# A hybrid decoder layer on one core: value projection 512 wide, a fifth weight buffer, the first y loaded earlier, and the last product in two banks

## The chip, the cores and the metric

The kernel runs on one core of a Trainium2 chip. The metric is the device time in microseconds (us) of one execution; runs are given by their median and their spread. The engines are TensorE (PE in the profile, with its weight loads as PEld), VectorE (DVE), ScalarE (ACT), GpSimd (POOL) and SyncE (SP), whose queue issues all DMAs of this kernel.

## The reference

One decoder layer over x of 2048 rows and 1024 channels, in float32. One projection of x by w_in (1024 x 3584) feeds three branches; their outputs y_A, y_B, y_C (256, 256 and 512 wide) are joined, multiplied by w_out (1024 x 1024), added to the scaled input and normalised:

```python
h = einsum('bsd,de->bse', x, w_in)
a_u, a_v, a_g, b_val, b_glu, b_g, c_q, c_f, c_i, c_g = split(h)
y_a = sgu(gelu(a_u), layernorm(gelu(a_v))) * silu(a_g)     # chunks of 128, masked 128x128 per head
y_b = silu(layernorm(conv31(b_val * sigmoid(b_glu)))) * silu(b_g)
y_c = hgrn2(c_q, c_f, c_i) * silu(c_g)                     # gated recurrence, chunks of 64, 4 heads
x = layernorm(ALPHA * x + concat(y_a, y_b, y_c) @ w_out) * g + b
```

## The kernel before, in words

**Split arithmetic.** Every large product is made of three matmuls: each operand is split into a high part (a cast on ACT, L145) and a low part (a subtraction on VectorE, L146), and `three` (L198 to L201) multiplies high by high, high by low and low by high into one PSUM bank. `load_split` loads a raw tile of 128x512 by DMA (L151) and splits it. Weights go to the rings `whi` and `wlo`, four tiles of 128x1024 each; x goes to `xhi` and `xlo`.

**Projections.** `proj_f` puts weights on the stationary side and 512 tokens on the moving side: 24 matmuls of 128x512 into one of three "mm" banks. `proj_t` puts 128 tokens on the stationary side and 256 weight columns on the moving side: 24 matmuls of 128x256. It serves `sgu_values` (a_v) and `values` (c_i). `values` (L341 to L347) goes over the 512 columns of c_i in two passes `vp` of 256, over the two groups of 512 tokens in a half, and over the four tiles of 128 tokens in a group; after each tile ACT copies the bank's 256 columns to `vh`.

**Stages.** The rows are taken in two halves of 1024 tokens. In the first: branch B (GLU, convolution of 31 taps on VectorE, L280 and L283), branch A (`sgu`), the values, branch C (`hgrn_unit`, four heads). In the second: branch B, the values, branch C, and branch A last. `sgu_setup` (first half) makes the masked weights and `abias` of branch A with some constants.

**The combinations of w_out.** During the first half `wo_steps` makes seven sums of blocks of w_out (four k tiles each, 28 blocks in all): it loads `wr` (L686), subtracts (L697), splits into `wsh` and `wsl` (two buffers each), and stores both to DRAM (L679). The last stage uses them as `wob`. A step is due every 2.5 units of a program clock, `later` and `tick`, which each group of three matmuls advances. The order on each engine is then set by the framework's scheduler, which works on the program order and the buffers.

**The last stage.** It goes over eight row pairs p, each of two tiles of 128 rows (`r1`, `r2` in `xr`). Seven products of 12 matmuls replace eight: a11, a12, a22 are quarters of y, and s1 to s4 are sums of quarters. `y_steps(p)` is a generator: it loads four quarters `ry` from DRAM (L821) into the ring of raw tiles, splits pair a (a11, a12), makes s1, s2, s3 (L845 to L847) and splits pair s (s2, s3), makes s4 (L850) and splits pair t (s1, s4), and splits b (a22). In row pair p the steps of p+1 (`ahead`) lie between the products. `plus` (L910) and `join` (L913) add products to the rows of x, `normed` takes mean and variance on ACT (L885 to L888) and `rstd_of` on POOL (L225, L226), and `store` (L876 to L880) normalises in two VectorE operations, subtract the mean times g (L877), then scale and add b (L879), and writes out. The last pair has its own order and takes its statistics on VectorE (`stats`, L891 to L903); its last product a22 is done in two halves of 256 columns into one bank `poe`. `free_c` is called in the last branch A after each unit: it loads `wob` into freed memory and takes the first two steps of y of pair 0.

Of the kernel before, what the change touches and what calls it, by code (L numbers as in the profile page):

```python
# [11 lines left out]
F32 = mybir.dt.float32  # L12
# [71 lines left out]
def _body(tc, nc, d, ctx):  # L84
# [19 lines left out]

    warm = cst.tile([P, G], BF16, name="warm")
    nc.vector.memset(warm, 0.0)
    wps = bank("sc", 2, "wps")
    for _ in range(NWARM):
        nc.tensor.matmul(wps, warm[:, :P], warm, start=True, stop=True)

# [53 lines left out]
    def load_small(nm, srcs):  # L164
        hi = wp.tile([P, 1024], F32R, tag="whi", bufs=4, name=f"wh_{nm}")
        lo = wp.tile([P, 1024], F32R, tag="wlo", bufs=4, name=f"wl_{nm}")
        load_split(f"w{nm}", hi, lo, srcs)
        return hi, lo
# [172 lines left out]
    def values(hf, xs, vh):  # L341
        for vp in range(2):
            ws = [load_w(d["wt"][1 + vp, j], f"ci{hf}_{vp}_{j}") for j in range(2)]
            for gi in range(GPH):
                for tt in range(4):
                    pt = proj_t(ws, xs[gi], tt, f"ci{hf}_{vp}_{gi}_{tt}")
                    nc.scalar.copy(vh[:, gi * 4 + tt, vp * 256 : (vp + 1) * 256], pt[:, :256])  # L347

# [231 lines left out]

    def sgu_setup():
# [3 lines left out]
        ones = cst.tile([P, 64], F32, name="ones")  # L585
        nc.gpsimd.memset(ones, 1.0)
        sb = cst.tile([P, 2, P], F32, name="sgub")
        nc.sync.dma_start(sb, d["sgub"])
        pr = bank("sc", 2, "rowsum").rearrange("p (a t) -> p a t", t=P)
        for hd in range(4):  # L590
            nc.tensor.matmul(pr[64 * (hd % 2) : 64 * (hd % 2) + 64, hd // 2, :], ones,
                             wm[:, hd, :], start=True, stop=True)
        for ft in range(2):
            nc.vector.scalar_tensor_tensor(abias[:, ft, :], pr[:, ft, :], vcol(V_SLB + ft),
                                           sb[:, ft, :], ALU.mult, ALU.add)
# [17 lines left out]
    def sgu_unit(g, gi, x, pl, vhat, w, after):  # L613
        if True:
            for ft in range(2):
                nm = f"{ft}_{g}"
                pu = proj_f(w[2 * ft], x, f"u{nm}")
                gu = pl.tile([P, G], F32, tag="gu", bufs=2, name=f"gu{nm}")
                nc.scalar.activation(gu, pu, AF.Gelu_apprx_tanh)
                pg = proj_f(w[2 * ft + 1], x, f"ag{nm}")  # L620
                sg = pl.tile([P, G], F32, tag="ag", bufs=2, name=f"agt{nm}")
                nc.scalar.activation(sg, pg, AF.Silu)
# [25 lines left out]
    def first_loads():  # L648
        wt = [[wp.tile([P, 1024], F32R, tag=t, bufs=4, name=f"{t}_first{k}")
               for t in ("whi", "wlo")] for k in range(2)]  # L650
# [80 lines left out]
    def sgu(hf, xs, pl, after):  # L731
        ws = [load_w(d["wt"][0, j], f"av{hf}_{j}") for j in range(2)]
        vhat = sgu_values(hf, xs, pl, ws)
        w = [load_wf(o, hf) for o in (A_U, A_G, A_U + 1, A_G + 1)]
        for gi in range(GPH):
            sgu_unit(hf * GPH + gi, gi, xs[gi], pl, vhat, w, after)

    for hf in range(NHALF):
# [8 lines left out]
        if hf == 0:  # L747
            lower_bounds()
            sgu_setup()
            with ExitStack() as esw:  # L750
                wo_start(pool("wos", stack=esw, reuse_waits="tile"))
                with ExitStack() as esa:
                    pl = pool(f"a{hf}", stack=esa, reuse_waits="tile")
                    sgu(hf, xs, pl, lambda gi, ft: None)
                values(hf, xs, vh)
                assert wo_done
        else:
            assert live[0] == 0
            esc.close()
            values(hf, xs, vh)  # L760
# [40 lines left out]
    n0, n1 = slice(0, 512), slice(512, 1024)  # L801
    ys, xr, first_y = {}, {}, []
    xrp = pool("xr", stack=es, side="right", reuse_waits="tile")

    def load_xr(p):
        xr[p] = []
        for k in range(2):
# [3 lines left out]
            xr[p].append(r)  # L811

    stiles = pool("stiles", stack=es, side="right")

    def y_steps(p):
        raw = []
        for k in range(2):
            for e in range(2):
# [56 lines left out]

    def store(t, r, rs, mv, parts):  # L876
        nc.vector.scalar_tensor_tensor(r, r, mv[:, 0:1], gb[:, 0, :], ALU.subtract, ALU.mult)  # L877
        for ns in parts:
            nc.vector.scalar_tensor_tensor(r[:, ns], r[:, ns], rs, gb[:, 1, ns], ALU.mult, ALU.add)  # L879
            nc.sync.dma_start(d["out"][t * P : (t + 1) * P, ns], r[:, ns])  # L880

    def normed(t, r):
# [29 lines left out]
    def join(r, ns, t):  # L912
        nc.vector.tensor_add(r[:, ns], r[:, ns], t)  # L913
# [113 lines left out]
```

## Time and profile before

| what | value |
|---|---|
| three runs | 937.88, 940.69, 938.23 us; median 938.23 |
| profiled execution | 939.29 us, span 937.6 us |
| granted TensorE clock | 0.996 |
| instructions | 15803 |
| HBM | 75.00 MB read, 31.46 MB written |
| first half, branches B and A | 0 to 147 us |
| values of the first half | 147 to 196.9 us, with the second pass from 172 |
| values of the second half | 455 to 501 us |
| output product | 767 to 930 us |

The profile is one execution. A line of it gives the engine, the line of the kernel, the operation, the tile written and the tiles read. Groups give the number of instructions, busy time and the mean ns of one; in the timeline a row begins with the start and the duration, and ends with the idle time before it and what ended it. Matmuls overlap, so that their spacing, start to start, and not their printed duration, is what they cost. "PE a <- DVE b" in the list of waits means that TensorE, about to write a, stood until VectorE had written b.

### The profile page before, as it was taken

What the parts mean: (1) busy time and instruction counts of PE and PEld (TensorE: products, weight loads), DVE (VectorE), ACT (ScalarE), POOL (GpSimd) and SP (SyncE); (2) the same over time, 40 slices, a digit from 0 to 9 for tenths busy, and PEclk for the clock granted to TensorE, in tenths of its full rate; (3) what the DMA queues carried; (4) which work ended last, traced back from release to release, by engine and by line L of the source; (5) the groups of instructions that cost most, each with busy time, mean ns of one, the idle gap of its engine ahead of it and who ended that gap; (6) DMA issues with size and microseconds to landing.
All of it is one profiled execution on the core that took longest, in us unless ns stands there. A gap on an engine that the chain in (4) does not pass through costs nothing. (4 is left out here: it accounts for less than half of the span.)

```text
span 937.6 us, 15803 instructions
## 1 busy us (share of the span) xinstructions
PE 911.4 (97%) x6057; PEld 752.4 (80%) x6057; DVE 712.9 (76%) x1614; ACT 393.7 (42%) x790; POOL 76.6 (8%) x127
## 2 busy tenths in 40 slices
PE   8999999999999999999999999999999999999995
PEld 5789888987777777788998777777788887777884
DVE  6998899826787669897998767778765235888787
ACT  6644353234354446543323445344443343334450
POOL 0001101000010000010000000001012001121112
PEclk9999999999999999999999999999999999999998
DMA  8756464111112104411211111111322687455422
GB/s 269 264 180 239 157 235 141 68 46 35 35 46 68 46 23 158 135 57 35 68 46 46 45 46 46 46 45 46 121 83 68 229 322 260 131 182 179 155 91 90
DMA packets 60812, 107.48 MB, mean 115 GB/s; under 512 B 5312, under 2 KB 21952, under 8 KB 60608
## 3 DMA queue, kind: packets, MB, share of 16 engines
q1 hardware_dynamic: 60736, 106.48, 33.5%
q8 instruction: 47, 0.77, 0.4%
q14 instruction: 29, 0.24, 0.1%
HBM read 75.00 MB, written 31.46 MB: 114 GB/s over the span
## 5 line engine op out<-in xcount | busy, mean ns | idle before, releaser
L283 DVE SCALAR_TENSOR_TENSOR acc<-bh,vec,acc 128x512 f32<-128x512 f32 x240 | 172.2, 743 | 2.2
L146 DVE TENSOR_TENSOR wl<-rw,wh 128x512 fp32r<-128x512 f32 x84 | 56.6, 684 | 29.4 <-ACT wh L145 29.4
L145 ACT CAST wh<-rw 128x512 fp32r<-128x512 f32 x84 | 50.1, 620 | 31.2 <-PE pm_f L200 11.1
L199 PE MATMUL pm_ci<-wh_ci,xhix 128*128 128x256 f32 x192 | 54.5, 284 | 0.0
L200 PE MATMUL pm_ci<-wl_ci,xhix 128*128 128x256 f32 x192 | 54.3, 283 | 0.0
L201 PE MATMUL pm_ci<-wh_ci,xlox 128*128 128x256 f32 x192 | 54.3, 283 | 0.0
L550 ACT ACTIVATE jk<-po 128x128 f32<-128x128 f32 x64 | 17.8, 278 | 60.7 <-PE po L545 59.8
L199 PE MATMUL pm_f<-xhix,wh 128*128 128x512 f32 x96 | 41.2, 429 | 0.0
L199 PE MATMUL pm_q<-xhix,wh 128*128 128x512 f32 x96 | 41.0, 427 | 0.0
L347 ACT COPY vh<-pm_ci 128x256 f32<-128x256 f32 x32 | 11.9, 373 | 65.6 <-PE pm_ci L201 65.6
L199 PE MATMUL pm_cg<-xhix,wh 128*128 128x512 f32 x96 | 39.0, 407 | 0.0
L200 PE MATMUL pm_q<-xlox,wh 128*128 128x512 f32 x96 | 39.0, 406 | 0.0
L201 PE MATMUL pm_q<-xhix,wl 128*128 128x512 f32 x96 | 37.9, 394 | 0.0
L201 PE MATMUL pm_f<-xhix,wl 128*128 128x512 f32 x96 | 37.8, 393 | 0.0
L200 PE MATMUL pm_f<-xlox,wh 128*128 128x512 f32 x96 | 37.6, 392 | 0.0
L201 PE MATMUL pm_cg<-xhix,wl 128*128 128x512 f32 x96 | 37.6, 392 | 0.0
L200 PE MATMUL pm_cg<-xlox,wh 128*128 128x512 f32 x96 | 37.5, 390 | 0.0
L199 PEld LDWEIGHTS pm_ci<-wh_ci,xhix 128*128 128x128 f32 x192 | 36.9, 192 | 0.0
L200 PEld LDWEIGHTS pm_ci<-wl_ci,xhix 128*128 128x128 f32 x192 | 36.9, 192 | 0.0
L201 PEld LDWEIGHTS pm_ci<-wh_ci,xlox 128*128 128x128 f32 x192 | 36.9, 192 | 0.0
L225 POOL TENSOR_SCALAR crs<-ss 128x4 f32<-128x4 f32 x16 | 3.6, 226 | 373.8 <-ACT jk L550 373.8
L438 DVE COPY_PREDICATED ST<-msk,sc 64x192 f32<-64x192 int32 (+2 forms) x96 | 28.8, 300 | 5.5 <-PE sc L432 3.2
(348 smaller groups left out, 2789.1 us busy)
## 6 DMA issues: line engine op xcount, KB each, us to landing
rw<-wf SPq DMA_DIRECT2D x84, 256.0 KB, 3.0
wob<-wo_dr SPq DMA_DIRECT2D x14, 1024.0 KB, 11.6
xr<-x SPq DMA_DIRECT2D x16, 512.0 KB, 4.5
ry<-y_dr SPq DMA_DIRECT2D x32, 256.0 KB, 3.9
out<-xr SPq DMA_DIRECT2D x15, 512.0 KB, 2.6
wo_dr<-wsh SPq DMA_DIRECT2D x28, 256.0 KB, 3.5
wo_dr<-wsl SPq DMA_DIRECT2D x28, 256.0 KB, 2.5
rx<-xT SPq DMA_DIRECT2D x24, 256.0 KB, 3.3
```

The lines of the kernel that those rows point to most:

```text
L145: nc.scalar.copy(hi, src)
L146: nc.vector.tensor_sub(lo, src, hi.bitcast(F32))
L199: nc.tensor.matmul(out, wh, xh, start=first, stop=False, **kw)
L200: nc.tensor.matmul(out, wh, xl, start=False, stop=False, **kw)
L201: nc.tensor.matmul(out, wl, xh, start=False, stop=last, **kw)
L225: nc.gpsimd.tensor_scalar(r, mv_var, scale, EPS, ALU.mult, ALU.add)
L283: nc.vector.scalar_tensor_tensor(a, h[:, k : k + G], vcol(cw + k), a, ALU.mult, ALU.add)
L347: nc.scalar.copy(vh[:, gi * 4 + tt, vp * 256 : (vp + 1) * 256], pt[:, :256])
L438: nc.vector.copy_predicated(ST[rr, :, 64 * m + j0 * b : 64 * m + (j0 + nj) * b], msk[rr, mo : mo + mw].unsqueeze(1).to_broadcast([64, 4, mw]),
L550: nc.scalar.activation(jk, po[:, c * P : (c + 1) * P], AF.Square, accum_out=ss[:, c : c + 1])
```

## The change

It has five parts.

1. `values` makes one pass of 512 columns with 128x512 matmuls. Its four weight tiles hold two k tiles of 512 columns each (`wi`, a new layout made on the host; `wt` keeps a_v).
2. The rings `whi` and `wlo` have five tiles (WB). The memory comes from the warm-up tile, `ones` and `sgub`, which go to pools of their own (`warm`, `sgs`) that are released; from `gu` and `ag`, which get one buffer; and from the DMA scratch, 1024 in place of 2048. The pool of the w_out combinations, opened next, takes over memory of `sgs`.
3. `y_steps` yields after its loads. Row pair 0 is loaded and its pair a split after the first unit of the last branch A, its pairs s and t follow after the third, where pair 1 is loaded too. In the loop the loads of p+2 are issued at the end of p.
4. The halves of the last a22 go to two banks, `poe` and `pof`.
5. `store` becomes `centre` and `finish`. In the last pair r1's `finish` stands behind the aggregate of r2 in the program.

```diff
+WB = 5
-        for vp in range(2):
-            ws = [load_w(d["wt"][1 + vp, j], f"ci{hf}_{vp}_{j}") for j in range(2)]
-            for gi in range(GPH):
-                for tt in range(4):
-                    pt = proj_t(ws, xs[gi], tt, f"ci{hf}_{vp}_{gi}_{tt}")
-                    nc.scalar.copy(vh[:, gi * 4 + tt, vp * 256 : (vp + 1) * 256], pt[:, :256])
+        ws = [load_w(d["wi"][j], f"ci{hf}_{j}") for j in range(4)]
+        for gi in range(GPH):
+            for tt in range(4):
+                pt = bank("mm", 3, f"pm_ci{hf}_{gi}_{tt}")
+                xs_ = slice(tt * P, (tt + 1) * P)
+                for kt in range(KT):
+                    wh, wl = [t.rearrange("p (k f) -> p k f", f=G)[:, kt % 2, :]
+                              for t in ws[kt // 2]]
+                    three(pt, xs[gi][0][:, kt, xs_], xs[gi][1][:, kt, xs_], wh, wl,
+                          kt == 0, kt == KT - 1)
+                    tick(0.64)
+                nc.scalar.copy(vh[:, gi * 4 + tt, :], pt)
...
-            sgu_setup()
+            with ExitStack() as est:
+                sgu_setup(pool("sgs", stack=est, reuse_waits="tile"))
...
-            if gi == 1:
-                first_y.append(y_steps(0))
-                for _ in range(2):
-                    next(first_y[0])
+            if gi == 0:
+                first_y.extend(y_steps(p) for p in range(2))
+                next(first_y[0])
+                next(first_y[0])
+            else:
+                next(first_y[0])
+                next(first_y[0])
+                next(first_y[1])
...
-        ahead = y_steps(p + 1)
+        ahead = first_y.pop(0) if first_y else None
...
             normed(2 * p, r1)
             if p + 2 < NP:
+                first_y.append(y_steps(p + 2))
+                next(first_y[0])
                 load_xr(p + 2)
...
-            d2 = bank("sc", 2, f"poe{p}")
+            d2 = bank("sc", 2, f"poe{p}"), bank("tr", 1, f"pof{p}")
...
-            store(2 * p, r1, rs1, mv1, [slice(0, DM)])
+            centre(r1, mv1)
             for k, ns in enumerate(halves):
-                product(d2, y["a22"], 6, True, ns)
-                join(r2, ns, d2[:, ns])
+                product(d2[k], y["a22"], 6, True, ns)
+                join(r2, ns, d2[k][:, ns])
                 take2(k + 1)
             rs2, mv2 = done2()
-            store(2 * p + 1, r2, rs2, mv2, (n0, n1))
+            finish(2 * p, r1, rs1, [slice(0, DM)])
+            centre(r2, mv2)
+            finish(2 * p + 1, r2, rs2, (n0, n1))
```

More of the change, by code (lines that the diff above doesn't have):

```diff
@@ L103, in bank @@
         return t
[L105 to L109, printed above, removed]
+    with ExitStack() as esw:
+        warm = pool("warm", stack=esw, side="right", reuse_waits="tile").tile([P, G], BF16, name="warm")
+        nc.vector.memset(warm, 0.0)
+        wps = bank("sc", 2, "wps")
+        for _ in range(NWARM):
+            nc.tensor.matmul(wps, warm[:, :P], warm, start=True, stop=True)
     ident = cst.tile([P, P], F32, name="ident")
@@ L164, in load_small @@
     def load_small(nm, srcs):
-        hi = wp.tile([P, 1024], F32R, tag="whi", bufs=4, name=f"wh_{nm}")
-        lo = wp.tile([P, 1024], F32R, tag="wlo", bufs=4, name=f"wl_{nm}")
+        hi = wp.tile([P, 1024], F32R, tag="whi", bufs=WB, name=f"wh_{nm}")
+        lo = wp.tile([P, 1024], F32R, tag="wlo", bufs=WB, name=f"wl_{nm}")
         load_split(f"w{nm}", hi, lo, srcs)
@@ L579, in _body, with sgu_setup @@
     abias = cst.tile([P, 2, P], F32, name="abias")
-    def sgu_setup():
+    def sgu_setup(tp):
         nc.sync.dma_start(wm, d["sguw"])
@@ L584, in sgu_setup @@
                                 fill=0.0, base=0, channel_multiplier=-1)
-        ones = cst.tile([P, 64], F32, name="ones")
+        ones = tp.tile([P, 64], F32, name="ones")
         nc.gpsimd.memset(ones, 1.0)
-        sb = cst.tile([P, 2, P], F32, name="sgub")
+        sb = tp.tile([P, 2, P], F32, name="sgub")
         nc.sync.dma_start(sb, d["sgub"])
@@ L617, in sgu_unit @@
                 pu = proj_f(w[2 * ft], x, f"u{nm}")
-                gu = pl.tile([P, G], F32, tag="gu", bufs=2, name=f"gu{nm}")
+                gu = pl.tile([P, G], F32, tag="gu", bufs=1, name=f"gu{nm}")
                 nc.scalar.activation(gu, pu, AF.Gelu_apprx_tanh)
                 pg = proj_f(w[2 * ft + 1], x, f"ag{nm}")
-                sg = pl.tile([P, G], F32, tag="ag", bufs=2, name=f"agt{nm}")
+                sg = pl.tile([P, G], F32, tag="ag", bufs=1, name=f"agt{nm}")
                 nc.scalar.activation(sg, pg, AF.Silu)
@@ L648, in first_loads @@
     def first_loads():
-        wt = [[wp.tile([P, 1024], F32R, tag=t, bufs=4, name=f"{t}_first{k}")
+        wt = [[wp.tile([P, 1024], F32R, tag=t, bufs=WB, name=f"{t}_first{k}")
                for t in ("whi", "wlo")] for k in range(2)]
@@ L731, in sgu @@
     def sgu(hf, xs, pl, after):
-        ws = [load_w(d["wt"][0, j], f"av{hf}_{j}") for j in range(2)]
+        ws = [load_w(d["wt"][j], f"av{hf}_{j}") for j in range(2)]
         vhat = sgu_values(hf, xs, pl, ws)
@@ L801, in _body @@
     n0, n1 = slice(0, 512), slice(512, 1024)
-    ys, xr, first_y = {}, {}, []
+    ys, xr, first_y, stiles = {}, {}, [], []
     xrp = pool("xr", stack=es, side="right", reuse_waits="tile")
@@ L811, in load_xr @@
             xr[p].append(r)
-    stiles = pool("stiles", stack=es, side="right")
     def y_steps(p):
@@ L824, in y_steps @@
                 raw.append(r)
+        yield
         a11, a12, a21, a22 = raw
@@ L828, in pair @@
         def pair(nm, srcs, names):
-            hi = wp.tile([P, 1024], F32R, tag="whi", bufs=4, name=f"wh_y{p}_{nm}")
-            lo = wp.tile([P, 1024], F32R, tag="wlo", bufs=4, name=f"wl_y{p}_{nm}")
+            hi = wp.tile([P, 1024], F32R, tag="whi", bufs=WB, name=f"wh_y{p}_{nm}")
+            lo = wp.tile([P, 1024], F32R, tag="wlo", bufs=WB, name=f"wl_y{p}_{nm}")
             n = srcs[0].shape[1]
@@ L837, in pair @@
                 out[name] = [t[:, sl].rearrange("p (k t) -> p k t", t=P) for t in (hi, lo)]
-        sa = stiles.tile([P, 1024], F32, tag="ysum", bufs=2, name=f"ysa{p}")
-        sb = stiles.tile([P, 1024], F32, tag="ysum", bufs=2, name=f"ysb{p}")
+        pair("a", (a11, a12), ("a11", "a12"))
+        yield
+        sa = stiles[0].tile([P, 1024], F32, tag="ysum", bufs=2, name=f"ysa{p}")
+        sb = stiles[0].tile([P, 1024], F32, tag="ysum", bufs=2, name=f"ysb{p}")
         s2, s3 = sa[:, :512], sa[:, 512:]
         s1, s4 = sb[:, :512], sb[:, 512:]
-        pair("a", (a11, a12), ("a11", "a12"))
-        yield
         nc.vector.tensor_add(s1, a21, a22)
@@ L853, in y_steps @@
         pair("b", (a22,), ("a22",))
+    stiles.append(pool("stiles", stack=es, side="right"))
     load_xr(0)
@@ L859, in _body @@
         sgu(NHALF - 1, xs, pl, free_c)
-    for _ in first_y[0]:
+    ot = pool("ot", stack=es, side="right", reuse_waits="tile")
+    for _ in first_y.pop(0):
         pass
-    ot = pool("ot", stack=es, side="right", reuse_waits="tile")
     gb = ot.tile([P, 2, DM], F32, name="gb")
@@ L874, in product, with centre, finish @@
             tick(0.64)
-    def store(t, r, rs, mv, parts):
+    def centre(r, mv):
         nc.vector.scalar_tensor_tensor(r, r, mv[:, 0:1], gb[:, 0, :], ALU.subtract, ALU.mult)
+    def finish(t, r, rs, parts):
         for ns in parts:
@@ L888, in normed @@
         nc.scalar.activation(jk, r, AF.Square, bias=nm, accum_out=mv[:, 1:2])
-        store(t, r, rstd_of(smp, mv[:, 1:2], 1, "ors", 1.0 / DM), mv, [slice(0, DM)])
+        rs = rstd_of(smp, mv[:, 1:2], 1, "ors", 1.0 / DM)
+        centre(r, mv)
+        finish(t, r, rs, [slice(0, DM)])
     def stats(t, r, parts):
@@ L982 @@
     "wf": ((NFT, P, KT * P), F32),
-    "wt": ((3, 2, P, 4 * 256), F32),
+    "wt": ((2, P, 4 * 256), F32),
+    "wi": ((4, P, 2 * 512), F32),
     "wout": ((P, KT, DM), F32),
@@ L1009 @@
         "wf": c(w.reshape(KT, P, NFT, P).transpose(2, 1, 0, 3).reshape(NFT, P, KT * P)),
-        "wt": c(tok.reshape(3, 2, 4, P, 256).transpose(0, 1, 3, 2, 4).reshape(3, 2, P, 1024)),
+        "wt": c(w[:, 256:512].reshape(2, 4, P, 256).transpose(0, 2, 1, 3).reshape(2, P, 1024)),
+        "wi": c(w[:, C_I * P : C_G * P].reshape(4, 2, P, 512).transpose(0, 2, 1, 3)
+                .reshape(4, P, 1024)),
         "wout": c(np.asarray(w_out)[0].reshape(KT, P, DM).transpose(1, 0, 2)),
@@ L1019 @@
     nc = _bacc.Bacc("TRN2", target_bir_lowering=False, num_devices=1,
-                    dynamic_dma_scratch_size=2048)
+                    dynamic_dma_scratch_size=1024)
     d = {n: nc.dram_tensor(n, s, t, kind="ExternalInput").ap() for n, (s, t) in _INS.items()}
```

1 line of the change is left out of this document (removed).

## The prediction

> **What bounds the kernel now.** I read the page first, then busy time by stage, then the waits of TensorE, then the timeline at the places that the change touches. The page's head and TensorE's row:
>
> ```profile
> span 937.6 us, 15803 instructions
> PE 911.4 (97%) x6057; PEld 752.4 (80%) x6057; DVE 712.9 (76%) x1614; ACT 393.7 (42%) x790; POOL 76.6 (8%) x127
> ```
>
> TensorE is busy 97% of the span, so time can come out in two ways only: fewer microseconds of matmul, or fewer of the 26 us in which it stands. Busy time by stage (columns: busy us and count on PE, PEld, DVE, ACT, POOL, then clock, DMA share, GB/s), for branch B's end with branch A and the weight combinations, for the eight row pairs of the output product, and for the end:
>
> ```profile
> 37.00:172.00 135.00, 133.51 (x817) 116.67 (x816) 127.08 (x225) 58.10 (x91) 12.41 (x23) 1.00 0.54 186
> ...
> 766.90:923.20 156.30, 153.42 (x665) 122.84 (x662) 119.50 (x153) 61.44 (x107) 23.41 (x28) 1.00 0.50 166
> 923.20:937.60 14.40, 3.53 (x25) 3.03 (x23) 8.96 (x16) 0.00 (x0) 3.04 (x2) 0.71 0.19 73
> ```
>
> The clock is 1.00 until the end, so nothing here hangs on it. TensorE's last 14.4 us hold 3.5 us of work: that stage is bound by the chain of the last row pair. In branch A, VectorE is nearly full too (127 of 135 us). The waits of TensorE that lie where the change works:
>
> ```profile
> PE poe L199 <- DVE xr L913: 3.2, 1, 3.2
> ...
> PE poz L199 <- DVE xr L910: 1.6, 2, 1.2
> ...
> PE pm_glu L200 <- DVE xlox L146: 1.0, 1, 1.0
> ...
> PE pod L201 <- DVE wl_y_s L146: 0.5, 1, 0.5
> ...
> PE pod L199 <- DMA wob<-wo_dr: 0.4, 1, 0.4
> ```
>
> **Values 512 wide.** 768 matmuls of 128x256 become 384 of 128x512 (the same columns in all), and 32 copies become 16. TensorE's timeline where the values end and the next projection begins, and in the output product, then the row of the copies:
>
> ```profile
> 194.76 0.28 PE L199 MATMUL pm_ci<-wh_ci,xhix 128*128 128x256 f32 x1
> ...
> 196.93 0.40 PE L199 MATMUL pm_f<-xhi_first,wh 128*128 128x512 f32 x1
> ...
> 197.62 0.40 PE L199 MATMUL pm_f<-xhi_first,wh 128*128 128x512 f32 x1
> 789.10 0.39 PE L199 MATMUL poz<-wob,wh_y_a 128*128 128x512 f32 x1
> ...
> 792.27 0.39 PE L201 MATMUL poa<-wob,wl_y_a 128*128 128x512 f32 x1
> L347 ACT COPY vh<-pm_ci 128x256 f32<-128x256 f32 x32 | 11.9, 373 | 65.6 <-PE pm_ci L201 65.6
> ```
>
> The length that a row prints (0.28, 0.40) overlaps the next matmul; what counts is start to start. From 194.76 to 196.93 are 18 matmuls: 2.17 / 18 = 0.1206 us each. 512 wide, from 196.93 to 197.62 are 3: 0.230; from 789.10 to 792.27 are 14: 0.2264. A 512-wide one thus costs about 12 ns less than two halves. Now 768 x 0.1206 = 92.6 us; then 384 x 0.230 = 88.3 or x 0.2264 = 86.9. The middle, 87.6, gives **-5.0** (bounds -4.3 and -5.7). All of it lies on the path, as TensorE does not wait in the values. The copies become about 0.6 us long (a 128x512 cast on ACT takes 0.62, row below), eight per half; three banks of 24 x 0.228 = 5.5 us hide them.
>
> [...]
>
> The four weights of the values now stay in use to the last tile, where two came free half way. The fifth buffer takes branch C's first weight ahead; the second is split after the values, two casts and two subtractions (0.62 and 0.68 each by the rows below, 2.6 us), behind the 5.5 us of the first projection. Zero; without that cover 2.6 us per half.
>
> **Start of branch B.** The `wos` pool takes over the memory of `sgs`, so the first load of w_out waits until `abias` is made. SyncE's order at the start, before:
>
> ```order
> L151 DMA rx_4_284<-xT 128x512
> L582 DMA wm<-sguw 128x512
> L588 DMA sgub<-sgub 128x256
> L151 DMA rx_5_284<-xT 128x512
> L686 DMA wr_0_658<-wout 128x1024
> L151 DMA rx_6_288<-xT 128x512
> L151 DMA rx_7_292<-xT 128x512
> ```
>
> and after:
>
> ```order
> L590 DMA wm<-sguw 128x512
> L596 DMA sgub<-sgub 128x256
> L153 DMA rx_5_288<-xT 128x512
> L153 DMA rx_6_292<-xT 128x512
> L153 DMA rx_7_296<-xT 128x512
> L153 DMA rw_0_0_397<-wf 128x512
> ```
>
> The last two x tiles no longer stand behind a 512 KB load. What that load does now, by the timelines of TensorE, SyncE, ACT and VectorE:
>
> ```profile
> 30.02 0.50 PE L200 MATMUL pm_glu<-xlox,whi_first 128*128 128x512 f32 x1 [0.98 <-DVE xlox L146]
> 19.33 0.43 SPq L686 DMA_DIRECT2D wr<-wout  x1
> 25.44 0.62 ACT L145 CAST wsh<-wr 128x512 fp32r<-128x512 f32 x1 [0.62 <-DMA wr<-wout]
> 26.75 0.68 DVE L146 TENSOR_TENSOR wsl<-wr,wsh 128x512 fp32r<-128x512 f32 x1
> ...
> 28.02 0.68 DVE L697 TENSOR_TENSOR wtb<-wr 128x512 f32<-128x512 f32 x1
> ...
> 29.28 1.28 DVE L146 TENSOR_TENSOR xlox<-rx,xhix 128x512 fp32r<-128x512 f32 x2
> ```
>
> xlox 6 and 7 come at 29.28 behind 1.4 us of w_out work and the wait for it, and TensorE stands 0.98 us before 30.02. Without w_out ahead they come over 1.2 us earlier: **-1.0** (bounds 0, if the x transfers are late by themselves, and -1.3, with a slower restart).
>
> In exchange all 28 blocks of w_out (cast, subtraction, two stores) fall between about 80 and 148 us, where 18 fall now. I price that at zero: TensorE waits for ACT's evictions there, which stand in the same queue as the casts, and three banks cover them. Its bound above is the slower rival.
>
> **y early, and the fifth buffer in the product.** The y of row pair 0 is loaded and split inside branch A, that of pair 1 is loaded there, and later ones a pair earlier. SyncE has a queue of these loads now, and TensorE two stalls at the first change of pair:
>
> ```profile
> 775.00 18.01 SPq L821 DMA_DIRECT2D ry<-y_dr  x6
> 794.10 0.50 PE L201 MATMUL pod<-wob,wl_y_s 128*128 128x512 f32 x1 [0.53 <-DVE wl_y_s L146]
> 798.83 0.50 PE L199 MATMUL poz<-wob,wh_y_s 128*128 128x512 f32 x1 [1.24 <-DVE xr L910]
> 796.90 1.28 DVE L877 SCALAR_TENSOR_TENSOR xr<-xr,omv,gb 128x1024 f32<-128x1024 f32 x1
> 798.10 0.68 DVE L910 SCALAR_TENSOR_TENSOR xr<-xr,poz 128x512 f32<-128x512 f32 x1
> ```
>
> VectorE's order in row pair 0 (xr_7232 and xr_7234 are its rows, xr_7236 the first row of pair 1), before:
>
> ```order
> L910 SCALAR_TENSOR_TENSOR xr_7234<-xr_7234,poz_8118 128x512 x2
> L913 TENSOR_TENSOR xr_7234<-xr_7234,pod_8120 128x512 x2
> L910 SCALAR_TENSOR_TENSOR xr_7232<-xr_7232,poz_8118 128x512
> L845 TENSOR_TENSOR ysb_8155<-ry_1_0_8150,ry_1_1_8152 128x512
> L847 TENSOR_TENSOR ysa_8154<-ry_0_0_8146,ry_1_0_8150 128x512
> L846 TENSOR_TENSOR ysa_8154<-ysb_8155,ry_0_0_8146 128x512
> L877 SCALAR_TENSOR_TENSOR xr_7234<-xr_7234,omv_8222,gb 128x1024
> L850 TENSOR_TENSOR ysb_8155<-ry_0_1_8148,ysa_8154 128x512
> L146 TENSOR_TENSOR wl_y_s<-ysa_8154,wh_y_s 128x1024
> ```
>
> and after (xr_6824 and xr_6826; pair 1's sums stand ahead of all this):
>
> ```order
> L926 SCALAR_TENSOR_TENSOR xr_6824<-xr_6824,poz_7718 128x512
> L929 TENSOR_TENSOR xr_6824<-xr_6824,poa_7719 128x512
> L148 TENSOR_TENSOR wl_y_s<-ysa_7778,wh_y_s 128x1024
> L926 SCALAR_TENSOR_TENSOR xr_6826<-xr_6826,poz_7718 128x512
> L148 TENSOR_TENSOR wl_y_t<-ysb_7779,wh_y_t 128x1024
> L926 SCALAR_TENSOR_TENSOR xr_6826<-xr_6826,poz_7718 128x512
> L929 TENSOR_TENSOR xr_6826<-xr_6826,pod_7720 128x512 x2
> ```
>
> wl_y_s of pair 1 is ready before pair 0's last products, and the four sums no longer lie between pair 0's joins and pair 1. That removes the waits at 794.10 and 798.83, 0.53 + 1.24 = 1.8 us. The stage has 156.3 us for some 660 matmuls of 0.228, which is 150.5: 5.8 us of stalls in all. The fifth buffer lets a pair's first split start without waiting for a buffer of the pair before. VectorE has 119.50 / 8 = 14.9 us of work per pair against TensorE's 84 x 0.228 = 19.15, so a pair can run almost without a stall where the order lets it. I take **-3.5**: the 1.8 and some two fifths of the other 4.0 (bounds -5.5, and +1 if the new order costs 0.15 a pair and gives nothing back). Pair 0's own splits move into branch A's second half: a few us of ACT and VectorE there, hidden as long as both have room, and at most the 1.8 back if they have none. The 0.4 for wob stays. `gu` and `agt` with one buffer each are rewritten a whole unit later, two projections of 5.5 us: zero.
>
> **The last product.** Timelines of VectorE, TensorE and POOL at the end:
>
> ```profile
> 926.33 1.27 DVE L879 SCALAR_TENSOR_TENSOR xr<-xr,orl,gb 128x1024 f32<-128x1024 f32 x1
> 927.51 0.41 DVE L913 TENSOR_TENSOR xr<-xr,poe 128x256 f32<-128x256 f32 x1
> 927.96 0.43 DVE L895 BATCH_NORM_STATS2 ost<-xr 128x6 f32<-128x256 f32 x1
> 927.98 0.39 PE L199 MATMUL poe<-wob,wh_y_b 128*128 128x256 f32 x1 [3.22 <-DVE xr L913]
> 930.00 0.42 DVE L913 TENSOR_TENSOR xr<-xr,poe 128x256 f32<-128x256 f32 x1 [1.61 <-PE poe L201]
> 930.91 0.24 DVE L899 BATCH_NORM_AGGREGATE omv<-ost 128x2 f32<-128x18 f32 x1
> 931.18 0.15 DVE L901 TENSOR_SCALAR orl<-omv 128x1 f32<-128x1 f32 x1
> 931.41 1.52 POOL L902 TENSOR_TENSOR orl<-orl,nhalf 128x1 f32<-128x1 f32 x1 [6.39 <-DVE orl L901]
> 932.97 1.41 DVE L879 SCALAR_TENSOR_TENSOR xr<-xr,orl,gb 128x512 f32<-128x512 f32 x2 [0.44 <-POOL orl L902]
> ```
>
> The second half waits for the join of the first, as both lie in one bank. VectorE's order there after the change:
>
> ```order
> L911 BN_STATS ost_8788<-xr_8640 128x6
> L929 TENSOR_TENSOR xr_8640<-xr_8640,poe_8790 128x256
> L929 TENSOR_TENSOR xr_8640<-xr_8640,pof_8791 128x256
> L911 BN_STATS ost_8788<-xr_8640 128x6 x2
> L893 SCALAR_TENSOR_TENSOR xr_8638<-xr_8638,orl_8861,gb 128x1024
> L915 BN_AGGR omv_8909<-ost_8788 128x2
> L917 TENSOR_SCALAR orl_8911<-omv_8909 128x1
> L889 SCALAR_TENSOR_TENSOR xr_8640<-xr_8640,omv_8909,gb 128x1024
> L893 SCALAR_TENSOR_TENSOR xr_8640<-xr_8640,orl_8911,gb 128x512 x2
> ```
>
> With two banks TensorE goes on at once, 3.2 us earlier at about 924.8, and is done at about 926.7; but row 1's L893 (1.2 us) now stands ahead of the aggregate. From 926.33: two joins at 0.45 (927.23), two stats at 0.46 (928.15), L893 (929.35), aggregate and epsilon 0.5 (929.85), POOL 1.52 and the hand-over (931.44), where 932.97 stands now: **-1.5** (bounds -0.8 if joins wait for TensorE, -2.2). Of the 3.2 us, about half is kept by VectorE's queue.
>
> **Sum.** -5.0 - 1.0 - 3.5 - 1.5 = -11.0. The profiled execution took 939.29 (span 937.6 and 1.7 around it), so 928.3; it stands 1.06 over the median of 938.23, so about **927.2** for the median.
>
> **Rivals.**
> 1. *The w_out blocks hold up branch A* (slower). From the trace's groups of wsh and its stores, of abias, and ACT's last gate:
>
> ```profile
> L679 SPq DMA_DIRECT2D wo_dr<-wsh x28: 319/353/1368, 32.2 to 140.3; - x28
> DMA to landing us min/median/max: 2.0/3.5/5.2
> 76.15 0.60 DVE L594 SCALAR_TENSOR_TENSOR abias<-rowsum,vec,sgub 128x128 f32<-128x128 f32 x2
> 148.31 0.60 ACT L622 ACTIVATE agt<-pm_ag 128x512 f32<-128x512 f32 x1
> ```
>
>    The first load goes out at 77 and lands about 82 (an estimate, with the longest landing). A block waits for the store of the block two before: 0.62 + 0.35 + 3.5 = 4.5 us for two, and 28 take 63 us, to 145: in time for the last agt (148.31), which stands behind the last block in ACT's order. At the longest landing it is 6.2 for two, to 168. Two banks of cover are 11 us, so it decides from (148 + 11 - 82) / 28 = 2.75 us per block. At 3.3 per block (174) TensorE would stand 15 us: **942**. For it: VectorE's full stage and the heavier DMA traffic. Against: the median landing. Chance 0.09.
> 2. *The product's pace is VectorE's.* If in each pair one 1.28 us operation falls ahead of the plus that frees poz, as at 796.90 now, TensorE loses 1.3 in seven pairs, +9 in place of -3.5: **939.5**. For it: VectorE's operations come in long pieces, and its order is fixed. Against: the four us of room per pair. Chance 0.07.
> 3. *The early y is hidden anyway*: the stalls move to another wait, the product gains 0 to 1 us. **930**. Chance 0.18.
> 4. *The 12 ns are not a matmul's own*: they come from something that both widths share per column, and one of 512 costs what two of 256 do. The values save nothing, **932**. The rows at two places contradict it; chance 0.04. [...]
>
> My forecast has 0.60, and 0.02 is left for gains elsewhere. About 0.3%, 2.8 us, is what a measurement here can tell from no change. Faster by more: 0.60 + 0.18 + 0.04 + 0.02 = 0.84; same (rival 2): 0.07; slower (rival 1): 0.09. The terms' lower ends add to -14.7, their upper ends to -4.1; with 1 us on each side for small stalls elsewhere that is 922.5 to 935, with rivals 3 and 4 inside and the first two outside (0.16).
>
> **What would show it.** Right: pm_ci 128x512 some 0.228 apart, 384 of them; no wait of 1 us for xlox near 30; poe's wait on L913 gone and the last L893 some 1.5 us nearer to the start of the last product; the product stage near 152.8 us. Wrong: TensorE waiting for ACT's gu or agt between 100 and 160 us (rival 1), for xr at every change of pair (rival 2), or the value stage not shorter by over 4 us (rival 4).

## The result, and the profile after

Over six runs each, the kernel before takes 939.13 us (937.55 to 940.69) and the changed one 934.38 us (933.51 to 935.1): a ratio of 0.9949, with a 95% interval of 0.9934 to 0.9964. That is 4.75 us faster, where 11.0 was forecast. The profiled execution takes 934.35 us with a span of 932.6, so 5.0 us of span against before.

Where they come from is seen by cutting both spans at the first matmul of each stage on TensorE (`pm_ci`, the first `pm_f` behind it, `poz`, `poe`):

| stage, us | before | after | difference | forecast |
|---|---|---|---|---|
| start to the first values | 147.53 | 146.62 | -0.9 | -1.0 |
| values, first half | 49.40 | 53.78 | **+4.4** | -2.5 |
| branch C, then branch B of the second half | 258.23 | 258.25 | 0 | 0 |
| values, second half | 46.07 | 43.52 | -2.5 | -2.5 |
| branches C and A, second half | 265.72 | 266.54 | +0.8 | 0 |
| output product, to `poe` | 156.22 | 151.64 | -4.6 | -3.5 |
| `poe` to the end | 14.41 | 12.27 | -2.1 | -1.5 |
| span | 937.58 | 932.61 | -5.0 | -11.0 |

Two stages went against the forecast. Branches C and A of the second half lost 0.8 us. The first half's values should have become 2.5 us shorter and became 4.4 longer, 6.9 us off: more than the whole shortfall of 6.0. The 0.9 us of the start can't be put down to the change: in another profile of the changed kernel (e11 below) the start takes 147.9 us, and in e4, which starts like the kernel before, 146.7. The waits of TensorE in the changed kernel, and the one that the kernel before has in the values:

```profile
PE bb L330 <- DVE bhn L324: 3.5, 1, 3.5
PE pst L531 <- DVE s L537: 2.7, 5, 0.9
...
PE pm_ci L202 <- DVE wl_ci L148: 1.2, 2, 1.0
...
PE pm_ci L201 <- ACT wh_ci L147: 1.0, 1, 1.0
```

```profile
PE bb L328 <- DVE bhn L322: 1.4, 1, 1.4
```

poe, poz, pod on wl_y_s and pm_glu on xlox are gone, as forecast. New are two waits of the values for their own weights, wh_ci and wl_ci, and the wait for bhn (the end of branch B's normalisation) that was 1.4 us before is 3.5 now. The chain that ended last, around 150 us (start, us, what), and then ACT's timeline at the same place, where the last value weight is cast:

```profile
145.60 4.35 DMA wo_dr<-wsh
...
150.02 0.62 ACT wsh L147
150.64 0.53 ACT wh_ci L147
...
151.19 0.04 DVE wl_ci L148
```

```profile
150.02 0.62 ACT L147 CAST wsh<-wr 128x512 fp32r<-128x512 f32 x1 [3.24 <-DMA wo_dr<-wsh]
150.55 0.61 ACT L147 CAST wh_ci<-rwci 128x512 fp32r<-128x512 f32 x1
...
152.97 0.61 ACT L147 CAST wh_ci<-rwci 128x512 fp32r<-128x512 f32 x1
```

ACT stood 3.24 us at the head of its queue for a w_out block, whose buffer was still being stored, and the value weight behind it could not be cast. The group of the blocks, its casts' releasers and the landing of its stores:

```profile
L687 SPq DMA_DIRECT2D wo_dr<-wsh x28: 319/382/413, 80.4 to 154.1; - x28
...
  DMA wo_dr<-wsh: 16.1, 11
  DVE wsl L148: 11.4, 6
...
DMA to landing us min/median/max: 2.0/3.3/6.2
```

28 stores between 80.4 and 154.1, so (154.1 - 80.4) / 27 = 2.73 us per block, with 16.1 us of ACT standing for landings, and 11.4 us until VectorE had subtracted an earlier block (wsl). Before, the first went out at 32.2 and the last at 140.3.

Last, TensorE's timeline behind the wait for bhn, and its clock (the column behind the count) in stretches of 2 us:

```profile
166.54 0.43 PE L202 MATMUL pm_ci<-wl_ci,xhi_first 128*128 128x512 f32 x1
166.77 0.63 PE L203 MATMUL pm_ci<-wh_ci,xlo_first 128*128 128x512 f32 x1
167.19 0.63 PE L201 MATMUL pm_ci<-wh_ci,xhi_first 128*128 128x512 f32 x1
...
170.18 0.40 PE L202 MATMUL pm_ci<-wl_ci,xhi_first 128*128 128x512 f32 x1
```

```profile
162.00:164.00 2.00, 0.00 (x0) 1.00 0.35 131
164.00:166.00 2.00, 0.89 (x4) 1.00 0.44 131
166.00:168.00 2.00, 2.00 (x8) 0.69 0.11 39
168.00:170.00 2.00, 2.00 (x6) 0.50 0.24 92
```

From 166.77 to 170.18 eight matmuls take 3.41 us, 0.426 each, where 17 from 172.01 to 175.87 take 0.227 each: the granted clock was half (0.50 from 168 to 170), and that costs 1.6 us more. So the stage's 53.8 us are 192 x 0.227 = 43.6 of matmul, 1.2 of transposes, 2.7 of steps that wait for weights (2.2 of idle time and the slower step around each), 4.1 for bhn with its restart, 1.6 of half clock and 0.6 of small things.

The tail, VectorE's and POOL's timeline, against the rows that the prediction shows:

```profile
923.05 0.41 DVE L929 TENSOR_TENSOR xr<-xr,poe 128x256 f32<-128x256 f32 x1
923.41 0.42 DVE L929 TENSOR_TENSOR xr<-xr,pof 128x256 f32<-128x256 f32 x1
923.75 0.75 DVE L911 BATCH_NORM_STATS2 ost<-xr 128x6 f32<-128x256 f32 x2
924.41 1.27 DVE L893 SCALAR_TENSOR_TENSOR xr<-xr,orl,gb 128x1024 f32<-128x1024 f32 x1
925.59 0.23 DVE L915 BATCH_NORM_AGGREGATE omv<-ost 128x2 f32<-128x18 f32 x1
...
927.65 1.42 DVE L893 SCALAR_TENSOR_TENSOR xr<-xr,orl,gb 128x512 f32<-128x512 f32 x2 [0.44 <-POOL orl L918]
```

From the first join to the last L893 4.6 us, where the prediction laid out 5.1: the narrow joins and statistics take 0.33 to 0.36 each and not 0.45.

### The profile page after: what moved, and what is told of

Read it like the earlier page. It is cut to its first block, busy times and chain, and to the rows that moved or that the text cites. A ratio compares the mean times of both kernels' runs of the same rounds, so it can differ in the third digit from the quotient of the medians.

```text
span 932.6 us, 15037 instructions
## 1 busy us (share of the span) xinstructions
PE 906.8 (97%) x5673; PEld 735.1 (79%) x5673; DVE 714.4 (77%) x1614; ACT 392.9 (42%) x774; POOL 82.1 (9%) x127
## 4 chain that ended last, share of the span: by engine, by line
PE 65%; DVE 17%; DMA 6%; ACT 4%; issue 4%; POOL 2%; SPq 0%; POOLq 0%; DVEq 0%; ACTq 0%
DVE acc L285 5%; PE pm_q L201 3%; PE poz L201 3%; PE pm_ci L203 3%; PE pm_ci L201 3%; PE pm_ci L202 3%; PE poz L203 3%; PE poz L202 3%; PE pm_q L203 3%; PE pm_q L202 3%; PE pm_f L201 3%; PE pm_f L203 2%; PE pm_f L202 2%; PE pm_cg L201 2%; PE pm_cg L203 2%
## 5 line engine op out<-in xcount | busy, mean ns | idle before, releaser
L201 PE MATMUL pm_ci<-wh_ci,xhix 128*128 128x512 f32 x96 | 37.3, 389 | 0.0
L202 PE MATMUL pm_ci<-wl_ci,xhix 128*128 128x512 f32 x96 | 37.3, 389 | 0.0
L203 PE MATMUL pm_ci<-wh_ci,xlox 128*128 128x512 f32 x96 | 37.3, 389 | 0.0
L355 ACT COPY vh<-pm_ci 128x512 f32<-128x512 f32 x16 | 9.4, 589 | 58.1 <-PE pm_ci L203 58.1
L537 DVE SCALAR_TENSOR_TENSOR s<-s,Tc,pst 128x128 f32<-128x128 f32 x56 | 19.4, 346 | 16.1 <-PE pst L531 15.9
L531 PEld LDWEIGHTS pst<-vh,KT 128*128 128x128 f32 x120 | 19.4, 188 | 14.5 <-DVE s L537 10.4
L503 ACT COPY ST<-sc 64x128 f32<-64x128 f32 x32 | 8.4, 261 | 50.9 <-PE sc L500 50.7
```

The lines of the kernel that those rows point to most:

```text
L201: nc.tensor.matmul(out, wh, xh, start=first, stop=False, **kw)
L202: nc.tensor.matmul(out, wh, xl, start=False, stop=False, **kw)
L203: nc.tensor.matmul(out, wl, xh, start=False, stop=last, **kw)
L355: nc.scalar.copy(vh[:, gi * 4 + tt, :], pt)
L503: nc.scalar.copy(ST[0:64, e:4:2, 64:128], pcv[64 * e : 64 * e + 64])
L531: pinned(nc.tensor.matmul(pst[:, cs], KT_[:, cs], V[:, c, :], start=True, stop=True))
```

## The experiments

Two theories stood at the start. **Late w_out**: the pool of the w_out combinations took over memory of `sgs`, so that its work began at 77 us in place of 19, was crowded into branch A, and held up the value weights and the convolution in the queues of ACT and VectorE. **Four weights at once**: a pass of 512 columns needs all four split weights within its first 5.5 us, wherever the w_out work lies. The stages of all runs, in us, from their profiles:

| kernel | start | values 1 | C, B | values 2 | C, A | product | end | span |
|---|---|---|---|---|---|---|---|---|
| before | 147.5 | 49.4 | 258.2 | 46.1 | 265.7 | 156.2 | 14.4 | 937.6 |
| after | 146.6 | 53.8 | 258.2 | 43.5 | 266.5 | 151.6 | 12.3 | 932.6 |
| e1 | 147.8 | 48.6 | 258.5 | 43.5 | 266.5 | 150.9 | 11.9 | 927.7 |
| e2 | 147.5 | 53.3 | 258.2 | 43.5 | 265.6 | 156.7 | 15.4 | 940.2 |
| e3 | 146.6 | 52.8 | 258.2 | 46.1 | 265.9 | 155.7 | 14.4 | 939.7 |
| e4 | 146.7 | 49.4 | 258.2 | 46.1 | 265.5 | 156.3 | 12.3 | 934.4 |
| e5 | 146.6 | 51.6 | 258.1 | 43.5 | 265.5 | 153.6 | 12.3 | 931.3 |
| e6 | 147.3 | 49.8 | 258.6 | 43.5 | 266.5 | 151.7 | 11.9 | 929.3 |
| e7 | 149.2 | 46.7 | 259.6 | 43.5 | 266.1 | 150.8 | 11.9 | 927.8 |
| e8 | 148.0 | 50.5 | 258.5 | 43.5 | 266.5 | 151.5 | 12.0 | 930.6 |
| e9 | 147.1 | 50.0 | 258.5 | 43.5 | 266.5 | 150.9 | 11.9 | 928.5 |
| e10 | 146.0 | 46.8 | 260.4 | 43.5 | 266.6 | 151.5 | 11.9 | 926.6 |
| e11 | 147.9 | 54.6 | 258.4 | 43.5 | 266.7 | 150.9 | 12.3 | 934.3 |

Runs came from several occasions, on which the kernel before took 939.1 to 940.8, so times are compared by their ratio to before.

**e1: w_out free of the constants.** On the kernel after:

```diff
-            with ExitStack() as est:
-                sgu_setup(pool("sgs", stack=est, reuse_waits="tile"))
             with ExitStack() as esw:
-                wo_start(pool("wos", stack=esw, reuse_waits="tile"))
+                wos = pool("wos", stack=esw, reuse_waits="tile")
+                with ExitStack() as est:
+                    sgu_setup(pool("sgs", stack=est, reuse_waits="tile"))
+                wo_start(wos)
```

> The kernel after, with the pool of the w_out combinations opened below the pool of sgu_setup's constants, so that the first load of w_out waits for nothing. Late w_out theory (the combinations, crowded between 80 and 154 us, hold up the splits of the value weights and the end of the convolution): the first half's value stage, 53.8 us, loses the 2.7 us of waits for wh_ci and wl_ci, about 2 of the 3.5 us wait for bhn and the 1.6 us of half clock behind it, and comes to 47 to 48 us; the wait for xlox near 30 us is back (1.3); time 934.4 - 6.3 + 1.3 = about 929.5. Rival, four weights at once (a 512-wide pass needs all four split weights within its first 5.5 us, wherever the w_out work lies): the waits for wh_ci and wl_ci stay, 2 to 3 us, and the time is 932 to 935.

Measured: 931.09 against 940.17, ratio 0.9893 (0.9875 to 0.9912). TensorE's waits:

```profile
PE bb L330 <- DVE bhn L324: 2.9, 1, 2.9
...
PE pm_glu L202 <- DVE xlox L148: 0.7, 1, 0.7
```

The waits for wh_ci and wl_ci are gone and the stage is back from 53.8 to 48.6 us; the wait for xlox is back. That is the late w_out theory. In this profile the clock is 1.00 from 148 to 174 us, also behind the wait for bhn; in e6 and e8, which change nothing in the first half, it is half for 3.4 us (0.52 and 0.63 in the 2 us stretches from 162 and 164 in e6, 0.50 and 0.65 from 164 and 166 in e8), and the stage takes 49.8 and 50.5 us. One part of it fell: the wait for bhn did not go to about 1.5 us but stayed at 2.9. It has another cause, tried in e7.

**e2: 512-wide values alone, on the kernel before** (the new `values` and its weight layout; four buffers).

> The kernel before with the 512-wide values alone: four weight buffers, w_out early, no other part of the change. Late w_out theory: no wait for wh_ci or wl_ci of more than 0.5 us, 2.5 us less in each value stage; but all four buffers are held to the end of the values, so branch C's first projection waits for its weights, by the estimate of 2.6 us per half: near zero in total, 936.5 to 940 against 939.1. Rival, four weights at once: a further 2 to 3 us of waits for wh_ci and wl_ci in each half, 941 or more.

Measured: 940.03 against 940.17, ratio 0.9997 (0.9985 to 1.0009). The waits, and VectorE's timeline behind them:

```profile
PE pm_ci L200 <- DVE wl_ci L146: 4.4, 3, 2.3
```

```profile
151.83 0.68 DVE L146 TENSOR_TENSOR wl_ci<-rwci,wh_ci 128x512 fp32r<-128x512 f32 x1
152.43 2.73 DVE L283 SCALAR_TENSOR_TENSOR acc<-bh,vec,acc 128x512 f32<-128x512 f32 x4
155.08 0.68 DVE L146 TENSOR_TENSOR wl_ci<-rwci,wh_ci 128x512 fp32r<-128x512 f32 x1
155.68 0.74 DVE L638 SCALAR_TENSOR_TENSOR mx<-mix,vec,abias 128x512 f32<-128x512 f32 x1
156.34 0.74 DVE L283 SCALAR_TENSOR_TENSOR acc<-bh,vec,acc 128x512 f32<-128x512 f32 x1
157.00 0.68 DVE L629 TENSOR_TENSOR gu<-gu,agt 128x512 f32<-128x512 f32 x1
157.60 0.68 DVE L146 TENSOR_TENSOR wl_ci<-rwci,wh_ci 128x512 fp32r<-128x512 f32 x1
```

With w_out early and four buffers the weights are late all the same: the last two get a buffer only when branch A's last weights give one up, and then their subtractions stand in VectorE's queue between taps. So four weights at once is right for four buffers, in the first half. The time lies in the range that the other theory gave, but not for its reason. The second half, with no branch A ahead of its values, has no such wait (43.5). And TensorE did not wait at the start of branch C in either half: the cost that the prediction feared without the fifth buffer, 2.6 us per half, is not there.

**e3: late w_out alone, on the kernel before.**

```diff
-            sgu_setup()
+            with ExitStack() as est:
+                sgu_setup(pool("sgs", stack=est, reuse_waits="tile"))
```

> The kernel before with the constants ones and sgub in a released pool whose memory the w_out pool takes over: only the first load of w_out moves, to behind abias at about 77 us. Late w_out theory: the wait for xlox near 30 us goes (-1.4), the last w_out block ends near 154 us, bhn is 2 us later, and if the wait grows to 3.5 us the clock is halved for some 3.3 us behind it: +1 to +3 in total, 940 to 942. Rival: -1.4, 937.7, with the value stage unchanged at 49.4 us.

Measured: 941.6 against 940.17, ratio 1.0012 (0.9999 to 1.0026). The interval reaches from no change to 0.3% slower. By stages of the profile, the first values lose 3.4, though they are still 256 wide and need two weights at a time; about 1.5 of that is half clock (18 matmuls of 128x256 take 3.65 us, from 153.38 to 157.03, where 18 x 0.1206 is 2.17). The start is 0.9 shorter, as it also is in e4 and e5, where w_out comes early. TensorE's timeline and ACT's:

```profile
152.09 0.39 PE L199 MATMUL pm_ci<-wh_ci,xhi_first 128*128 128x256 f32 x1 [1.89 <-ACT gu L619]
```

```profile
148.98 0.62 ACT L145 CAST wsh<-wtb 128x512 fp32r<-128x512 f32 x1 [5.32 <-DMA wo_dr<-wsh]
149.51 0.62 ACT L145 CAST wh_ci<-rwci 128x512 fp32r<-128x512 f32 x1
150.14 1.28 ACT L619 ACT_TABLE_LOAD   x1
151.44 0.60 ACT L619 ACTIVATE gu<-pm_u 128x512 f32<-128x512 f32 x1
```

Here the blocks reached what the first rival of the prediction named: TensorE wanted the bank that the eviction gu had not yet freed, since ACT had stood 5.32 us for a store. Moving w_out alone costs 3.4 us in this stage.

**e4: two banks alone, on the kernel before** (part 4 and 5 of the change).

> The kernel before with the last product's halves in two banks and r1's finish behind the aggregate, nothing else. Theory from the two profiles (VectorE's queue keeps part of TensorE's 3.2 us): from the first matmul of poe to the end of the span 12.3 us in place of 14.4, so -2.2, 936.9. Rival (all of TensorE's wait comes back): -3.2, 935.9. Second rival (finish ahead of the aggregate costs as much as is won): 0, 939.1.

Measured: 937.73 against 940.17, ratio 0.9976 (0.9963 to 0.9989), so 2.3 us; the end of the span is 12.3 us in place of 14.4, as expected of VectorE's queue.

**e5: e1 with four buffers.**

```diff
-WB = 5
+WB = 4
```

> The kernel of e1 with four weight buffers in place of five. Theory now (both conditions count: the value weights are late when w_out is late, and when the third and fourth weight must wait for branch A's last weights to free a buffer): waits for wl_ci of 4 to 5 us in the first half's values as in e2, with the clock halved behind them, value stage 52 to 53.5 us in place of 48.6; product stage unchanged at 151 to 152 us if the early y alone had removed its stalls, 153 to 155 if the fifth buffer had a part in it; time 5 to 8 us above e1. Rival (w_out early is all that the value weights need): value stage 48.6.

Measured: 935.18 against 940.77, ratio 0.994 (0.9919 to 0.9961).

```profile
PE pm_ci L202 <- DVE wl_ci L148: 4.2, 3, 2.3
```

The waits of e2 are back: with w_out early, the fifth buffer's part in the values is to let their own last weights be split in time. The first values take 51.6 us, a little less than expected, and the product 153.6, between 156.2 and 150.9; by the ratios the time is about 4 us above e1's, where 5 to 8 were expected. This kernel keeps the single buffers of `gu` and `agt` and the smaller DMA scratch, which no run takes back alone; its start and its branches C and A are as short as e4's, so they show no cost.

**e6: e1 with y late** (`free_c`, `y_steps` and the loop as before).

```diff
-        ahead = first_y.pop(0) if first_y else None
+        ahead = y_steps(p + 1)
...
-                first_y.append(y_steps(p + 2))
-                next(first_y[0])
```

> The kernel of e1 with the y steps as in the kernel before (row pair 0 loaded and half split after the third unit of the last branch A, later pairs loaded inside the row pair ahead), still with five buffers and two banks. Theory (the early loads and splits removed the product's stalls): product stage 155 to 156.5 us in place of 150.9, with waits for wh_y_s, wl_y_s and for xr at the first change of pair; branch C and A of the second half 0.8 us shorter (265.7); time 4 us above e1. Rival (the fifth buffer did it): product stage 151 to 152 us.

Measured: 930.9 against 940.77, ratio 0.9891 (0.9856 to 0.9926). The product takes 151.7 us: the rival is right. With four buffers and y late it is 156.2, y early alone makes 153.6 (e5), the fifth buffer alone 151.7, both 150.9 to 151.6. The fifth buffer does most of it by itself, and the two don't add up. Branches C and A of the second half stay at 266.5, so the 0.8 us lost there do not come from the early y; they are absent only with four buffers (265.5 to 265.9 in before and e2 to e5).

**e7: e1 with the normalisation later.**

```diff
-DTAP, DNORM, DWO = (1.5, 1.35), 8.0, 2.5
+DTAP, DNORM, DWO = (1.5, 1.35), 10.0, 2.5
```

> The kernel of e1 with the parts of branch B's normalisation spaced 10 program-clock units apart in place of 8 (DNORM), which puts the transposes bb behind 75 matmuls of the values in place of 48. Theory (TensorE now reaches bb before VectorE, full with taps, has made bhn; only the place of bb in TensorE's order is wrong): the wait for bhn near 162 us (3.1) goes, value stage 45.5 us, time 3 us under e1. Rival (VectorE is the bound of this stage, and whatever stands next in TensorE's order waits for it): the 3 us come back at another place of the value stage or at the start of branch C.

Measured: 929.69 against 940.77, ratio 0.988 (0.9856 to 0.9905). The wait for bhn falls from 2.9 to 1.0 and the stage from 48.6 to 46.7; but the next stage takes 1.1 us more, and a wait of 2.5 us for pst appears near 692 us. More than half of it came back in the next stage; the start is 1.3 us longer in this profile, which the edit doesn't explain. e1 and e7 are not told apart by their intervals.

**e8: e1 with finish first.**

```diff
             centre(r1, mv1)
+            finish(2 * p, r1, rs1, [slice(0, DM)])
...
-            finish(2 * p, r1, rs1, [slice(0, DM)])
```

> The kernel of e1 with r1's finish put back ahead of the joins of the last two halves, its place in the kernel before; the two banks stay. Theory (the tail is VectorE's queue, which has the same work in either order): from the first matmul of poe to the end 11.9 to 12.3 us as in e1, same time. Rival (the place of finish was part of the gain): 13 us or more, 1.2 us slower.

Measured: 931.45 against 940.77, ratio 0.9899 (0.9871 to 0.9927). The end takes 12.0 us, as in e1 (11.9): where finish stands does not matter, VectorE's sum of work does. Of the 2.0 us that this execution takes longer in the first values, 1.6 are 3.4 us at half clock, by the rate of the changed kernel; more of it under e9.

**e9: w_out behind x, and still early.** On e1:

```diff
+                if j == 0:
+                    nc.gpsimd.tensor_copy(r[:, :1], x[:, KT - 1, :1].bitcast(F32))
                 nc.sync.dma_start(r, d["wout"][:, j + 4 * e, :])
```

> The kernel of e1 with one more thing: a one-column copy on POOL from the last xlox tile into the first wr tiles, so that the first load of w_out goes out behind the last x tile (near 25 us) and not ahead of it. Theory (both gains can be had together: x first, and w_out still some 50 us earlier than in the kernel after): no wait for xlox near 30 us (0.85 us in e1), first values stage 48 to 49 us as in e1 (up to 50.5 if the clock is halved there), time 0.8 to 1.3 us under e1, some 928.5 where the kernel before takes 939.1. Rival (w_out is the bound of the stage even from 25 us on): waits for wh_ci or wl_ci come back, no gain on e1.

Measured: 930.62 against 940.14, ratio 0.9891 (0.9869 to 0.9914). The first load goes out at 27.6, TensorE does not wait for xlox (nor does it in e4 to e6, where w_out stands ahead), and no weight is late. The profile's first values take 50.0 us and not 48.6, for the clock. Clock of e9, then of e1, behind a wait for bhn of nearly the same length (2.80 and 2.87):

```profile
162.00:164.00 2.00, 1.87 (x6) 0.52 0.17 67
164.00:166.00 2.00, 2.00 (x8) 0.63 0.36 131
166.00:168.00 2.00, 2.00 (x10) 1.00 0.00 0
```

```profile
162.00:164.00 2.00, 1.25 (x6) 1.00 0.42 131
164.00:166.00 2.00, 2.00 (x10) 1.00 0.22 74
166.00:168.00 2.00, 2.00 (x10) 1.00 0.15 57
```

e9 ran some 3.4 us at half clock, e1 not at all. Its gain on e1 is not told apart by the ratios.

**e10: e9 with the normalisation later in the first half only** (DNORM 10 and 8).

> The kernel of e9 with the parts of branch B's normalisation 10 units apart in the first half (8 in the second). Theory: as in e7 the wait for bhn in the first values falls from 3 to about 1.2 us, too short for the clock to be halved, and by a spacing unchanged in the second half e7's new wait of 2.7 us for pst near 692 us does not come: 1 us under e9. Rival (VectorE's queue is the bound there): what is won in the values is lost at the start of branch C, same time as e9.

Measured: 928.1 against 940.14, ratio 0.9869 (0.9849 to 0.9889). The wait for bhn is 1.1 us, the clock is 1.00 from 148 to 174 us, and the first values take 46.8 us; 1.8 us of that go back into the next stage (260.4). Its median is the lowest of the study, but its interval overlaps those of e1 and e6 to e9. On the chip of this run its interval and that of the changed kernel (e11) do not overlap.

**e11: the changed kernel again**, on the chip of e9 and e10.

> The changed kernel itself, on the chip of e9 and e10. If the cause found is right it takes 934 to 935 where the kernel before takes 939, 5 to 6 us more than e9, with the waits for wl_ci, wh_ci and bhn in the first values again, each time the same, and the clock halved behind them for about 3.4 us.

Measured: 934.77 against 940.14, ratio 0.9936 (0.992 to 0.9952). The same waits stand in the first values (by stretches, TensorE stands 1.8 us from 152 to 156 us, where weights were late, and 3.5 from 162 to 168, where bhn was). The clock is halved behind them for 6.8 us (0.85, 0.50 and 0.50 in the 2 us stretches from 164, 166 and 168, 0.72 from 170 to 174), twice as long as expected, and the stage takes 54.6 us.

## Why the prediction was wrong

The sign was right and the size was not: 4.75 us and not 11.0. The time of 934.38 lies inside the stated range (922.5 to 935), near its upper end, and that is luck: the values gave +1.9 us where their bounds were -4.3 and -5.7, and the room that the other terms had left covered it, as product and end together came out 1.7 us better than forecast.

- **The step that failed** is the one on the w_out blocks: "I price that at zero: TensorE waits for ACT's evictions there, which stand in the same queue as the casts, and three banks cover them." In the changed kernel the banks did cover the evictions. But the evictions are not all that stands behind the blocks. The value weights' casts and subtractions stand in the same queues, and they have no cover, because the 512-wide pass needs all four at once. e1 takes away the lateness alone and wins 5.2 us of stage; e3 adds it alone and loses 3.4. Of this 1.6 and 1.5 us are half clock.
- **The pace of the blocks** was mis-sized. The prediction reckoned 4.5 us for two, so 2.25 each, and an end at 145 us; measured were 2.73 each and an end at 154, at a median landing of 3.3 us in place of 3.5. The 11.4 us that ACT stood for VectorE's subtractions have no term in that sum. Nor did the rival's limit of 2.75 us per block decide: at (154.4 - 81.2) / 27 = 2.71 in e3, TensorE stood for an eviction all the same. What cost time was one long stand of ACT, 3.24 us in the changed kernel and 5.32 in e3, just when TensorE needed what came behind it.
- **"All of it lies on the path, as TensorE does not wait in the values"** was wrong as well. The trace of before has a wait of 1.37 us there, for bhn near 161 us. It is VectorE's, so faster matmuls run into it. In e1, with w_out early again, it is 2.9 us, and the first half keeps 0.8 of its 2.5 us; in e6 and e8, with the half clock, nothing. e7 and e10 shorten the wait to 1.0 and 1.1 and reach 46.7 and 46.8 us, all that was forecast for this stage, but 1.1 to 1.8 us go back into the next one. The second half has no such neighbour, and its 2.55 us came out at 43.52 / 192 = 0.227 us per matmul, where two of 256 took 46.07 / 192 = 0.240.
- **The clock** was left out: "nothing here hangs on it". In the changed kernel the half clock behind the wait of 3.50 us cost 1.6 us more, and in e11 about 3, an estimate by the same rate over 6.8 us.
- **The fifth buffer** was given the wrong work. It was to load branch C's first weight ahead, and its loss was to cost 2.6 us per half; e2 and e5 show no wait there. It is needed for the last value weights (4.2 to 4.4 us without it) and it is worth 4.5 us in the product by itself (e6), where the prediction took 1.8 us for two waits that the early y removes and 1.7 for everything else. With five buffers the early y adds at most 0.8.
- **Product and end** came out at -4.6 of -3.5 and -2.1 of -1.5, the end for the reason given (e4). The start's -0.9 of -1.0 looks right but is not shown to be the change's. The wait for xlox was 0 to 1.0 us in kernels whose w_out load stands ahead of x (none in e4, e5 and e6, 0.7 in e1, 1.0 in before), so that this term is chance in part or in whole.
- **Elsewhere** the second half's branches C and A lose 0.8 us with five buffers. TensorE's waits for pst grow from 1.7 to 2.7 us there. Which of VectorE's operations moved ahead of them was not tried, and stays open.

Rival 1 was the right mechanism with the wrong victim. It was priced by one queue's evictions, so that its chance of 0.09 meant a loss of 15 us or nothing, when the runs show a loss of 3.4 (e3) to 5.2 us (e1) in the stage.

## What to carry to other kernels

When memory is found for one buffer by letting pools follow each other, look at what the next pool's first transfer now waits for, and at everything that stands behind the late work in each engine's queue (ACT stood 3.24 us here, 5.32 in e3), not only at what TensorE waits for today. A wider pass needs its whole set of operands at its first tile (here four split weights within 5.5 us): check that the buffers and the splits of all of them come before it. A wait that seems harmless can set the floor for a stage as soon as its matmuls become faster: the one for bhn was 1.37 us in the kernel before and 2.87 in e1.

## What the runs showed of the hardware that was not expected

TensorE's granted clock fell to half behind some idle times and not behind others. It did so for 3.4 us behind one idle time of 1.89 us in e3, 2.5 in e6, 2.80 in e9, 2.9 in e8 and 3.50 in the changed kernel, but it stayed at 1.00 behind 2.87 in e1, 1.37 in the kernel before and 1.08 in e10. In e11, behind 3.5, the slow stretch was 6.8 us by the clock column, and so it was in the first values of e2, behind 2.3 and 1.55. Eight matmuls of 128x512 at half clock took 3.41 us in the changed kernel in place of 1.82, so 1.6 more; 18 of 128x256 around the stretch in e3 took 3.65 in place of 2.17, so 1.5 more.

What decides whether the clock falls is not shown: e1 and e9 differ in it behind idle times of 2.87 and 2.80 us, and it fell behind 1.89 in e3. The rows of e3, 1 us each:

```profile
150.00:151.00 1.00, 0.20 (x2) 1.00 0.58 225
151.00:152.00 1.00, 0.00 (x0) 1.00 1.09 238
152.00:153.00 1.00, 0.92 (x7) 1.00 0.90 326
153.00:154.00 1.00, 1.00 (x9) 0.76 0.90 340
154.00:155.00 1.00, 1.00 (x7) 0.50 0.65 246
155.00:156.00 1.00, 1.00 (x6) 0.50 1.06 408
156.00:157.00 1.00, 1.00 (x7) 0.53 0.84 258
```
